# Last mixer of a two-model kernel: convolution taps added up by accumulating DMAs, all weights split, keys turned inside the value products

## The chip, the cores and the metric

The kernel runs on one core of a Trainium2 chip. Its time is the device time of one execution, in microseconds; the median of three executions before the change is 1564.31 us (1563.68 to 1568.18). A profiled execution of its own has a trace with the start and the duration of every instruction on every engine. The engines are named as in a profile: PE (TensorE's matmuls), PEld (its weight loads), DVE (VectorE), ACT (ScalarE), POOL (GpSimd) and SP (SyncE, which issues the weight loads from HBM).

## The reference

Two transformer-like models run one after the other on 256 tokens of width 1024: the first has two layers, the second has one layer, whose mixer is the last mixer of the program. It is the only part that the change touches:

```python
z = _rmsnorm(h, mix_norm[i]) @ w_in[i]
conv_a, conv_gt, q, k, v, r, g_lr = jnp.split(z, SPLIT_POINTS, axis=-1)
y_conv = _conv_module(conv_a, conv_gt, conv_w[i], conv_b[i], conv_ln_g[i], conv_ln_b[i])
y_gla = _gla(q, k, v, r, g_lr, gate_w_up[i], gate_b[i], gla_norm[i])
h = h + jnp.concatenate([y_conv, y_gla], axis=-1) @ w_out[i]
```

`_conv_module` forms `glu = a * sigmoid(b)` in 512 channels, runs a causal convolution of 31 taps along the tokens in each channel by itself, adds a bias, and applies a layer norm and SiLU. `_gla` is a gated linear attention in chunks of 64 tokens with four heads: decays are the exponential of a running sum of log-sigmoids, scores are taken inside each chunk, a state is handed from chunk to chunk, and its output has a norm and a gate `silu(r)`.

## The kernel before

All weights lie in one flat HBM tensor, in units of 128 x 1024 float32 (512 KB). SP loads one unit after the other into five staging buffers (tile `st`, line 179). A unit is normally *split* for an exact product in the fast format of PE: ACT casts it to the high half (`whi`, L158), DVE subtracts that from the unit and leaves the low half (`wlo`, L161), and activations are split likewise. A product of a weight block with the activations is then three matmuls (`mm3`: high by high, high by low, low by high; L276 to L278). The halves have seven buffers each. In the last mixer some units are used *raw*: the staged float32 block is multiplied directly with a float32 copy of the normalised input (`n.f32`, eight ACT instructions, L1159), one float32 matmul in place of three (L273, L348). The value weights and the output gate's weights are raw (`RAW_V`, `RAW_R`), the query and key weights are split.

The mixer runs in this order: eight units for `conv_a` and `conv_gt`, four times two (`conv_in` then forms `glu` for 128 channels, a quarter of them); one unit for the low-rank decay gate; two for queries and two for keys; four value units (`vproj`); the scores of four heads; the keys turned (four transposes of `ke` on PE, copied to `kt` by ACT, L1248 and L1249); three state products (L1256); the first half of the output gate (`output_gate(0)`, L273); the products of scores and states with values (L1307, L1311); the second half of the gate with the norm of the attention's output between its blocks (`o_norm`: column sums on PE, a power on POOL, L497; `o_scale`: eight diagonal matrices made by ACT, L506, and spread by PE, L516); then `w_out`, first with the four attention parts (`ys[4]` to `ys[7]`), then with the four convolution parts.

The taps of the convolution are background work, in a list `b.bg`; each weight unit that is asked for takes `b.rate` entries from it. Of 31 taps, DVE does 19 for each quarter in `tap`, each on top of the sum so far (`yc`, L1151; the first is ACT's, L1148). The other 12 (`NA`) are multiplied by ACT (`tap2`, two instructions for two quarters, L1143), and DVE adds the product to `yc` (L1144). When the second part of `w_out` is asked for, what is left in the list is issued and `conv_norm` follows: `centre` (column sums over the channels by PE, L1276; subtract, L1278; squares, L1280), `variance` (L483, a power, two diagonals), `scale` (L1291, SiLU L1292, split L372 and L373).

The order on each engine isn't that of the code: a scheduler at build time puts instructions of all engines in an order by when it expects them to be ready. On the chip each engine runs its list in that order and an instruction that waits holds up all behind it. Chores (`b.after`) are issued when so many blocks of matmuls have been issued. POOL runs three powers in this mixer and one small load.

Of the kernel before, what the change touches and what calls it, by code (L numbers as in the profile page):

```python
# [19 lines left out]
P = 128  # L20
# [14 lines left out]

RATE, R_QK, R_V, R_R, R_O, NA = 5, 5, 9, 10, 5, 12

RAW_QK, RAW_V, RAW_R = False, True, True

CONV_AT, CONV_WAIT, CONV_SQ, CONV_RMS = 1, 0, 6, 6  # L40
GATE_AT, O_SUM, O_SPREAD = 12, 4, 6

# [25 lines left out]
class Norm:  # L68
# [3 lines left out]
    def __init__(self, b, h2, finish):  # L72
        self.b, self.h2, self.finish = b, h2, finish
        self.f32 = None
        self.sq = [None, None]
        self.state = 0
        self.gap = 12
        self.waiting = []

    def __call__(self, k):  # L80
        return self.h2[:, k, :, :], self.f32 and self.f32[:, k, :]

# [42 lines left out]
class Builder:  # L125
# [38 lines left out]
    def wtile(self):  # L164
        return tuple(self.wpool.tile([P, UW], F32R, tag=t, name=t) for t in ("whi", "wlo")) + (None,)

# [8 lines left out]

    def unit(self, *slabs, raw=False):

        st, src = self.staged(slabs)
        self.nc.sync.dma_start(st, src)
        if raw:  # L180
            self.run_bg(self.raw_rate)
            return None, None, st
        w = self.wtile()
        self.halves(st, w, slice(0, UW))
        self.run_bg()
        return w
# [62 lines left out]

    def colunit(self, name, l, cols, raw=False):  # L250
        return self.unit(*self.colspec(name, l, cols), raw=raw)

# [9 lines left out]

    def vunit(self, name, l, u, c0, raw=False):
        return self.unit(raw=raw, *[(name, l, slice(k * P, (k + 1) * P), slice(c0, c0 + 512)) for k in (2 * u, 2 * u + 1)])


    def mm3(self, ps, w, b, a, first, last):

        hi, lo, raw = w
        s = slice(b * P, (b + 1) * P)  # L270
        mm = self.nc.tensor.matmul
        if raw is not None:
            mm(ps, raw[:, s], a[1], start=first, stop=last, skip_group_check=True)  # L273
        else:
            a = a[0]
            mm(ps, hi[:, s], a[:, 0, :], start=first, stop=False, skip_group_check=True)  # L276
            mm(ps, hi[:, s], a[:, 1, :], start=False, stop=False, skip_group_check=True)  # L277
            mm(ps, lo[:, s], a[:, 0, :], start=False, stop=last, skip_group_check=True)  # L278
        self.tick()

    def mmw(self, bank, w, b, a, first, last):


        hi, lo, _ = w
        s = slice(b * P, (b + 1) * P)
        a = a[0]
        mm = self.nc.tensor.matmul
        mm(bank[:, 0, :], lo[:, s], a[:, 0, :], start=first, stop=False, skip_group_check=True)  # L288
        mm(bank, hi[:, s], a, start=False, stop=last, skip_group_check=True)  # L289
        self.tick()  # L290
# [39 lines left out]

    def vproj(self, name, l, c0, h, raw=False):

        banks = [self.psw.tile([P, 512], F32, tag="bank", name="bank") for _ in range(2)]
        mm = self.nc.tensor.matmul
        for u in range(ND // 2):
            hi, lo, w = self.vunit(name, l, u, c0, raw)
            order = [(kk, t) for kk in range(2) for t in range(2)]
            if u == ND // 2 - 1:
                order.sort(key=lambda kt: kt[1])
            for kk, t in order:  # L340
                k = 2 * u + kk
                a2, a = h(k)
                ah, al = a2[:, 0, :], a2[:, 1, :]
                c = slice(kk * 512, (kk + 1) * 512)
                first, last = k == 0, k == ND - 1
                s = slice(t * P, (t + 1) * P)
                if raw:
                    mm(banks[t], a[:, s], w[:, c], start=first, stop=last)  # L348
                    continue
                mm(banks[t], ah[:, s], hi[:, c], start=first, stop=False)  # L350
                mm(banks[t], ah[:, s], lo[:, c], start=False, stop=False)  # L351
                mm(banks[t], al[:, s], hi[:, c], start=False, stop=last)  # L352
                self.tick(2)
# [14 lines left out]
    def split(self, src, name="a"):  # L368
# [4 lines left out]
        nc.vector.tensor_tensor(a[:, 1, :], src, a[:, 0, :].bitcast(F32), op=ALU.subtract)  # L373
        return a, None

# [123 lines left out]

    def diags(self, col, n, act=False):  # L500

        dg = []
        for i in range(n):
            d = self.small.tile([P, P], F32, tag="dg", name="dg")
            if act:
                self.nc.scalar.mul(d, self.ident, col[:, i:i + 1])  # L506
            else:
                self.spread = self.nc.vector.tensor_scalar_mul(d, self.ident, col[:, i:i + 1])
            dg.append(d)
        return dg  # L510

    def bcast(self, dg):

        ps = self.psw.tile([P, 512], F32, tag="bank", name="bank")
        for i, d in enumerate(dg):
            self.nc.tensor.matmul(ps[:, i * P:(i + 1) * P], self.ones, d, start=True, stop=True)  # L516
        return ps[:, 0:len(dg) * P]

# [121 lines left out]
def two_block_kernel(ctx: ExitStack, tc: tile.TileContext, x_in, mem_in, p_in, params, sinks, table, onehot,  # L640
# [360 lines left out]
    def embedding():  # L1001
# [3 lines left out]
        for k in range(2):  # L1005
            a = b.work.tile([P, 2, T], F32R, tag="sum", name="pk", bufs=4)
            nc.scalar.copy(a[:, 0, :], pin[:, k, :])
            nc.vector.tensor_tensor(a[:, 1, :], pin[:, k, :], a[:, 0, :].bitcast(F32), op=ALU.subtract)
            pk.append((a, None))
        pu.extend(b.rowunit("ple_w_proj_2", 0, slice(k * P, (k + 1) * P)) for k in range(2))  # L1010
# [7 lines left out]
    with tc.tile_pool(name="ple", bufs=1) as pp:  # L1018
# [4 lines left out]
        def products(bank, t, h, w, c, first, last):  # L1023
            s = slice(t * P, (t + 1) * P)
            ah, al = h[0][:, 0, s], h[0][:, 1, s]
            mm(bank, ah, w[0][:, c], start=first, stop=False)
# [76 lines left out]
def _gla_mixer(b, n, n2, gain, x, gate_up, cst, updater):  # L1103
# [3 lines left out]
    with b.acts(8), tc.tile_pool(name="gla", bufs=1) as gp:  # L1107
# [8 lines left out]
        nc.gpsimd.memset(reset[:, :, 0:1], 0.0)  # L1116
        n.f32 = gp.tile([P, ND, T], F32, tag="h32", name="h32")

        def cu(c, raw=False):
            return b.colunit("w_in_2", 0, slice(c, c + P), raw)  # L1120


        glu = gp.tile([P, 4, T + NT - 1], F32, tag="glu", name="glu")
        nc.gpsimd.memset(glu[:, :, 0:NT - 1], 0.0)
        yc = gp.tile([P, 4, T], F32, tag="yc", name="yc")
        cw = gain("conv_w_2", 4 * NT)
        cb = gain("conv_b_2", 4)

        def conv_in(i, bank):
# [4 lines left out]
            nc.vector.tensor_tensor(glu[:, i, NT - 1:], t[:, 0, :], sg, op=ALU.mult)  # L1134
            b.bg += [lambda j=j: tap(i, j) for j in range(NT - NA)]
            if i % 2:
                b.bg += [lambda j=j: tap2(i - 1, j) for j in range(NT - NA, NT)]

        def tap2(i, j):

            t = gp.tile([P, 2, T], F32, tag="tap", name="tap", bufs=2)
            for e in range(2):
                nc.scalar.mul(t[:, e, :], glu[:, i + e, j:j + T], cw[:, 4 * j + i + e:4 * j + i + e + 1])  # L1143
            nc.vector.tensor_tensor(yc[:, i:i + 2, :], yc[:, i:i + 2, :], t, op=ALU.add)  # L1144

# [9 lines left out]
        for i in range(4):  # L1155
            bank = b.proj([cu(o + i * P) for o in (0, 512)], n, kouter=(i == 0))[0]
            n.then(lambda i=i, bank=bank: conv_in(i, bank))
        for d in range(ND):
            nc.scalar.mul(n.f32[:, d, :], x[:, d, :], gain("mix_norm_2")[:, d:d + 1])  # L1159


        b.rate = b.raw_rate = R_QK
        ug = b.unit(*[("w_in_2", 0, slice(k * P, (k + 1) * P), (2560, 16)) for k in range(ND)])
# [37 lines left out]
        k = b.work.tile([P, 2, T], F32, tag="sum", bufs=4, name="k")  # L1201
        bank = b.proj([cu(1024 + e * P, RAW_QK) for e in range(2)], n)[0]
        nc.vector.scalar_tensor_tensor(q, bank, 0.125, b.rb2(n), op0=ALU.mult, op1=ALU.mult)
        bank = b.proj([cu(1280 + e * P, RAW_QK) for e in range(2)], n)[0]
        nc.vector.tensor_tensor(k, bank, b.rb2(n), op=ALU.mult)
# [4 lines left out]
        qd, qu, kd, ku, ke = (prods[i] for i in ("qd", "qu", "kd", "ku", "ke"))  # L1210


        b.rate = b.raw_rate = R_V
        v = gp.tile([P, 2, 512], F32, tag="v", name="v")
        for t, bank in enumerate(b.vproj("w_in_2", 0, 1536, n, RAW_V)):
            nc.scalar.mul(v[:, t, :], bank, n.rt[:, t:t + 1])
# [4 lines left out]
        def output_gate(i):  # L1221
            bank = b.proj([cu(2048 + (2 * i + e) * P, RAW_R) for e in range(2)], n)[0]
            rr = b.work.tile([P, 2, T], F32, tag="sum", bufs=4, name="gu")
# [15 lines left out]
        for h in range(4):  # L1239
            scores(h)  # L1240
        b.rate = b.raw_rate = R_R


        kt = gp.tile([P, 2, 2, P], F32, tag="t1", name="kt")
        ps = b.psw.tile([P, 2, 2, P], F32, tag="bank", name="bank")
        for t in range(2):
            for a in range(2):
                nc.tensor.transpose(ps[:, t, a, :], ke[:, a, t * P:(t + 1) * P], b.ident)  # L1248
        nc.scalar.copy(kt, ps)  # L1249
        st = gp.tile([P, 3, 2, P], F32, tag="state", name="state")  # L1250
# [71 lines left out]
        def o_scale(rt):  # L1322
            for i in range(2):
                ps = b.bcast(b.diags(rt[:, 4 * i:4 * i + 4], 4, act=True))
                for e in range(2):
# [12 lines left out]
        def part(j, i):  # L1338
            def f():
                b.rate = R_O  # L1340
                w = b.rowunit("w_out_2", 0, slice(i * P, (i + 1) * P))
                if j == CONV_AT:
                    b.run_bg(len(b.bg))
                    conv_norm()
# [98 lines left out]
```

## Time and profile before

| | |
|---|---|
| median of three executions | 1564.31 us |
| the profiled execution's own time | 1567.1 us |
| its span from the first instruction to the last | 1565.3 us |
| PE busy in the span | 1541.1 us |
| DVE busy | 1211.2 us |
| ACT busy | 884.2 us |
| POOL busy | 28.1 us |
| share of the chain that ended last: PE, DVE, ACT | 94%, 3%, 2% |

A row names the line, the engine, the operation and the tiles (out<-in). Times of a stretch are counted from the span's start. PE's matmuls overlap, so a row's duration is longer than the distance between two starts. The granted clock of PE is 1.00 at 2.4 GHz; at its lower level, 1.2 GHz, it would be 0.5, and a stretch with both lies between. The last mixer takes PE from about 1224.6 us to 1341.8 us, where the next feed-forward's first matmul starts.

### The profile page before, as it was taken

What the parts mean: (1) busy time and instruction counts of PE and PEld (TensorE: products, weight loads), DVE (VectorE), ACT (ScalarE), POOL (GpSimd) and SP (SyncE); (2) the same over time, 40 slices, a digit from 0 to 9 for tenths busy, and PEclk for the clock granted to TensorE, in tenths of its full rate; (3) what the DMA queues carried; (4) which work ended last, traced back from release to release, by engine and by line L of the source; (5) the groups of instructions that cost most, each with busy time, mean ns of one, the idle gap of its engine ahead of it and who ended that gap; (6) DMA issues with size and microseconds to landing.
All of it is one profiled execution on the core that took longest, in us unless ns stands there. A gap on an engine that the chain in (4) does not pass through costs nothing.

```text
span 1565.3 us, 23488 instructions
## 1 busy us (share of the span) xinstructions
PE 1541.1 (98%) x8896; PEld 1341.4 (86%) x8896; DVE 1211.2 (77%) x2039; ACT 884.2 (56%) x1530; POOL 28.1 (2%) x41
## 2 busy tenths in 40 slices
PE   8999999999999999999999999999999999999997
PEld 7888887888888888888788888888888968888886
DVE  7977788878776787778687877778776897877774
ACT  7555546556555555554655655555555557555553
POOL 1000000000000000000000000000000000000000
PEclk9999999999999999999999999999999999999999
DMA  8655464427554666547352755447554524565542
GB/s 285 217 182 189 158 219 135 161 98 252 191 192 133 212 217 195 191 144 242 133 179 87 245 188 188 139 167 247 188 183 142 203 73 142 172 219 189 195 153 90
DMA packets 78418, 279.11 MB, mean 178 GB/s; under 512 B 8986, under 2 KB 10042, under 8 KB 78304
## 3 DMA queue, kind: packets, MB, share of 16 engines
q1 hardware_dynamic: 76176, 273.19, 52.7%
q0 software_dynamic: 1120, 3.36, 0.6%
q8 instruction: 70, 1.15, 0.3%
q10 hardware_dynamic: 1008, 1.05, 0.2%
q14 instruction: 44, 0.36, 0.1%
HBM read 276.50 MB, written 1.07 MB: 177 GB/s over the span
## 4 chain that ended last, share of the span: by engine, by line
PE 94%; DVE 3%; ACT 2%; DMA 1%; issue 0%; POOL 0%; ACTq 0%; POOLq 0%; SPq 0%; DVEq 0%
PE bank L289 44%; PE bank L288 23%; PE abank L289 9%; PE abank L288 5%; DMA st<-wflat 1%; PE bank L350 1%; PE bank L348 1%; PE bank L352 1%; PE bank L351 1%; PE bank L276 1%; PE bank L277 1%; PE bank L278 1%; PE bank L273 1%; DVE x L679 1%; PE bank L483 0%; PE bank L516 0%
## 5 line engine op out<-in xcount | busy, mean ns | idle before, releaser
L289 PE MATMUL bank<-h,whi 128*128 128x512 f32 x2416 | 847.3, 393 | 0.0
L288 PE MATMUL bank<-h,wlo 128*128 128x256 f32 x2416 | 679.4, 281 | 7.2 <-DVE wlo L161 7.2
L161 DVE TENSOR_TENSOR wlo<-st,whi 128x1024 fp32r<-128x1024 f32 (+1 forms) x515 | 612.7, 1208 | 63.0 <-ACT whi L158 62.6
L158 ACT CAST whi<-st 128x1024 fp32r<-128x1024 f32 (+1 forms) x515 | 532.2, 1041 | 152.5 <-DMA st<-wflat 97.4
L289 PEld LDWEIGHTS bank<-h,whi 128*128 128x128 f32 x2416 | 452.1, 187 | 100.4 <-DVE h L432 0.3
L288 PEld LDWEIGHTS bank<-h,wlo 128*128 128x128 f32 x2416 | 456.5, 189 | 12.1 <-DVE wlo L161 6.8
L327 ACT COPY sum<-bank 128x256 f32<-128x256 f32 x310 | 114.1, 370 | 284.9 <-PE bank L289 284.5
L289 PE MATMUL abank<-a,whi 128*128 128x512 f32 x624 | 222.2, 393 | 0.0
L328 DVE TENSOR_TENSOR sum<-bank,sum 128x256 f32<-128x256 f32 x310 | 130.3, 423 | 113.4 <-ACT sum L327 112.8
L289 PE MATMUL bank<-a,whi 128*128 128x512 f32 x624 | 218.1, 393 | 0.0
L288 PE MATMUL bank<-a,wlo 128*128 128x256 f32 x624 | 175.0, 281 | 0.0
L288 PE MATMUL abank<-a,wlo 128*128 128x256 f32 x624 | 174.8, 282 | 0.0
L289 PEld LDWEIGHTS bank<-a,whi 128*128 128x128 f32 x624 | 116.8, 187 | 26.4
L289 PEld LDWEIGHTS abank<-a,whi 128*128 128x128 f32 x624 | 116.7, 187 | 26.0
L288 PEld LDWEIGHTS bank<-a,wlo 128*128 128x128 f32 x624 | 117.9, 189 | 1.4 <-DVE pt L618 0.8
L288 PEld LDWEIGHTS abank<-a,wlo 128*128 128x128 f32 x624 | 117.6, 189 | 1.0 <-issue 0.8
L546 DVE TENSOR_TENSOR sum<-sum,rb 128x512 f32<-128x512 f32 x132 | 90.8, 691 | 3.4
L372 ACT CAST a<-a 128x256 fp32r<-128x256 f32 x132 | 53.3, 407 | 55.9 <-DVE a L550 55.8
L373 DVE TENSOR_TENSOR a<-a,a 128x256 fp32r<-128x256 f32 x132 | 55.1, 421 | 26.8 <-ACT a L372 26.7
L548 ACT ACTIVATE sg<-sum 128x256 f32<-128x256 f32 x132 | 54.4, 415 | 32.3 <-DVE sum L546 32.2
L550 DVE TENSOR_TENSOR a<-sg,sum 128x256 f32<-128x256 f32 x132 | 55.0, 420 | 7.4 <-ACT sg L548 6.8
L679 DVE SCALAR_TENSOR_TENSOR x<-bank,x 128x256 f32<-128x256 f32 x80 | 33.1, 421 | 35.0 <-PE bank L289 34.0
(273 smaller groups left out, 1240.7 us busy)
## 6 DMA issues: line engine op xcount, KB each, us to landing
st<-wflat SPq DMA_DIRECT2D x515, 512.0 KB, 4.2
tb<-fd POOLq DMA_DIRECT2D x4, 512.0 KB, 4.0
x<-x_in SPq DMA_DIRECT2D x4, 256.0 KB, 4.4
mem<-mem_in SPq DMA_DIRECT2D x4, 256.0 KB, 8.7
st<-wflat ACTq DMA_DIRECT2D x4, 128.0 KB, 5.9
st<-wflat SPq DMA_DIRECT2D x4, 128.0 KB, 4.0
gf<-last_gain POOLq DMA_DIRECT2D x1, 512.0 KB, 5.5
out_dram<-y ACTq DMA_DIRECT2D x2, 256.0 KB, 2.6
```

Of the source, the lines that this page charges most:

```text
L158: hi = self.nc.scalar.copy(w[0][:, s], st[:, s])
L161: lo = self.nc.vector.tensor_tensor(w[1][:, s], st[:, s], w[0][:, s].bitcast(F32), op=ALU.subtract)
L288: mm(bank[:, 0, :], lo[:, s], a[:, 0, :], start=first, stop=False, skip_group_check=True)
L289: mm(bank, hi[:, s], a, start=False, stop=last, skip_group_check=True)
L327: self.nc.scalar.copy(dst, banks[c][:, 1, :])
L328: self.nc.vector.tensor_tensor(dst, banks[c][:, 0, :], dst, op=ALU.add)
L372: nc.scalar.copy(a[:, 0, :], src)
L373: nc.vector.tensor_tensor(a[:, 1, :], src, a[:, 0, :].bitcast(F32), op=ALU.subtract)
L546: nc.vector.tensor_tensor(gu, gu, self.rb2(n), op=ALU.mult)
L548: nc.scalar.activation(sg, gu[:, 0, :], AF.Silu)
L550: nc.vector.tensor_tensor(a, sg, gu[:, 1, :], op=ALU.mult)
L679: nc.vector.scalar_tensor_tensor(x[:, d, :], bank[:, e, :], scale, x[:, d, :], op0=ALU.mult, op1=ALU.add)
```

## The change

Of the 31 taps ACT now multiplies 18 and DVE 13. DVE no longer adds ACT's products: the first product of each pair of quarters is written straight into a tile `yd`, and each of the other 17 goes into one of four buffers `tap`, from which a DMA issued by POOL adds it to `yd` in SBUF. The two pairs have a `yd` each, so there are 2 x 17 such DMAs, and each waits for the one before it on the same `yd`. `conv_rest` adds both `yd` to `yc` at the end. No unit is raw any more, so the value and gate weights are split by ACT and DVE and take three matmuls a block, and `n.f32` goes. The keys are turned by a chore inside the value products. The eight diagonals of the output norm become two DVE instructions of 128 x 512 and two matmuls of that width. The rates at which background work is issued are lower.

```diff
-RATE, R_QK, R_V, R_R, R_O, NA = 5, 5, 9, 10, 5, 12
-RAW_QK, RAW_V, RAW_R = False, True, True
+RATE, R_QK, R_V, R_R, R_O, NA = 3, 2, 4, 5, 5, 18
-GATE_AT, O_SUM, O_SPREAD = 12, 4, 6
+GATE_AT, TURN_AT, O_SUM, O_SPREAD = 12, 16, 6, 5
...
+        yd = [gp.tile([P, 2, T], F32, tag=f"yd{p}", name="yd") for p in range(2)]
+        taps2 = [[], []]
...
-            b.bg += [lambda j=j: tap(i, j) for j in range(NT - NA)]
+            b.bg += [lambda j=j: step(i, j) for j in range(NT - NA)]
             if i % 2:
-                b.bg += [lambda j=j: tap2(i - 1, j) for j in range(NT - NA, NT)]
-        def tap2(i, j):
-            t = gp.tile([P, 2, T], F32, tag="tap", name="tap", bufs=2)
+                taps2[i // 2].extend(range(NT - NA, NT))
+        def step(i, j):
+            tap(i, j)
+            p = max(range(2), key=lambda p: len(taps2[p]))
+            if taps2[p]:
+                tap2(p, taps2[p].pop(0))
+        def conv_rest():
+            b.run_bg(len(b.bg))
+            for p in range(2):
+                while taps2[p]:
+                    tap2(p, taps2[p].pop(0))
+            for p in range(2):
+                ycp = yc[:, 2 * p:2 * p + 2, :]
+                nc.vector.tensor_tensor(ycp, ycp, yd[p], op=ALU.add)
+        def tap2(p, j):
+            t = yd[p] if j == NT - NA else gp.tile([P, 2, T], F32, tag="tap", name="tap", bufs=4)
             for e in range(2):
-                nc.scalar.mul(t[:, e, :], glu[:, i + e, j:j + T], cw[:, 4 * j + i + e:4 * j + i + e + 1])
-            nc.vector.tensor_tensor(yc[:, i:i + 2, :], yc[:, i:i + 2, :], t, op=ALU.add)
+                i = 2 * p + e
+                nc.scalar.mul(t[:, e, :], glu[:, i, j:j + T], cw[:, 4 * j + i:4 * j + i + 1])
+            if t is not yd[p]:
+                nc.gpsimd.dma_start(yd[p], t, accum_op=ALU.add)
...
-        for d in range(ND):
-            nc.scalar.mul(n.f32[:, d, :], x[:, d, :], gain("mix_norm_2")[:, d:d + 1])
...
+        def turn():
+            ps = b.psw.tile([P, 2, 2, P], F32, tag="bank", name="bank")
+            for t in range(2):
+                for a in range(2):
+                    nc.tensor.transpose(ps[:, t, a, :], ke[:, a, t * P:(t + 1) * P], b.ident)
+            nc.scalar.copy(kt, ps)
+        b.after(TURN_AT, turn)
...
-                ps = b.bcast(b.diags(rt[:, 4 * i:4 * i + 4], 4, act=True))
+                dg = gp.tile([P, 4, P], F32, tag="odg", name="dg", bufs=2)
+                nc.vector.tensor_tensor(dg, b.ident.unsqueeze(1).to_broadcast([P, 4, P]),
+                                        rt[:, 4 * i:4 * i + 4].unsqueeze(2).to_broadcast([P, 4, P]), op=ALU.mult)
+                ps = b.bcast([dg.rearrange("p c q -> p (c q)")], 4 * P)
...
                 if j == CONV_AT:
-                    b.run_bg(len(b.bg))
+                    conv_rest()
                     conv_norm()
```

The scheduler moves instructions as well. On POOL, in the last mixer before, two powers (`r<-v`, with 8 and 2 columns) follow each other with nothing between them:

```order
L1116 MEMSET reset_12478 128x8
L497 TENSOR_TENSOR r_12550<-v_12549,mhalf_88 128x2
L497 TENSOR_TENSOR r_13300<-v_13299,mhalf_88 128x8
L497 TENSOR_TENSOR r_13448<-v_13447,mhalf_88 128x2
```

After, on the same place of POOL, 34 accumulating DMAs stand among them; `yd_12484` is the first pair of quarters and `yd_12485` the second. These are the rows around the 8-column power, of which 22 DMAs stand ahead of it and 12 behind it:

```order
L1147 DMA yd_12485<-tap_12998 128x512
L1147 DMA yd_12484<-tap_13083 128x512
L1147 DMA yd_12485<-tap_13073 128x512
L484 TENSOR_TENSOR r_13423<-v_13422,mhalf_88 128x8
L1147 DMA yd_12485<-tap_13078 128x512
L1147 DMA yd_12484<-tap_13111 128x512
L1147 DMA yd_12485<-tap_13088 128x512
L1147 DMA yd_12484<-tap_13121 128x512
```

From the start of the list the DMAs stand thus: nine on the first pair; two times one on the second pair and one on the first; seven on the second; one on each; the power; five times one on each; two on the second; the 2-column power.

On ACT the decay (from `z`, the gate's pre-activation, to `eend`, the last of its exponentials) stood in one piece before:

```order
L1181 ACTIVATE z<-bank,pc 128x256 x2
L1183 ACTIVATE az<-z 128x512
L1184 ACT_TABLE_LOAD
L1184 ACTIVATE az<-az 128x512
L1185 ACT_TABLE_LOAD
L1185 ACTIVATE az<-az 128x512
L1194 ACT_TABLE_LOAD
L1194 ACTIVATE epos<-cum 128x512
L1195 ACTIVATE eneg<-cum 128x512
L1197 ACTIVATE eend<-dl 128x512
```

After, four pairs of taps and three casts stand inside it (the three exponentials `epos`, `eneg` and `eend` follow the last row):

```order
L1182 ACTIVATE z<-bank,pc 128x256
L1145 ACTIVATE tap<-glu,pc 128x256 x2
L1182 ACTIVATE z<-bank,pc 128x256
L156 CAST whi<-st 128x1024
L1184 ACTIVATE az<-z 128x512
L1145 ACTIVATE tap<-glu,pc 128x256 x2
L1185 ACT_TABLE_LOAD
L1185 ACTIVATE az<-az 128x512
L1145 ACTIVATE tap<-glu,pc 128x256 x2
L1186 ACT_TABLE_LOAD
L1186 ACTIVATE az<-az 128x512
L156 CAST whi<-st 128x1024 x2
```

On PE the convolution's norm (L1276 is the centring, L483 the variance's sums, L516 the spreading of the scale) had the attention's `w_out` products (`abank`) after the centring and between its later steps. Of 96 such products all stood behind the centring:

```order
L516 MATMUL bank<-dg,ones 128x128 x3
L1276 MATMUL bank<-yc,ones 128x256
L516 MATMUL bank<-dg,ones 128x128
L1276 MATMUL bank<-yc,ones 128x256
L516 MATMUL bank<-dg,ones 128x128 x2
L1276 MATMUL bank<-yc,ones 128x256 x2
L276 MATMUL abank<-a_13350,whi 128x256 x4
```

After, the first pair's centring (L1282) stands 13 products ahead of their end, and the second pair's centring, the sums (L470) and the spreading (L500) follow each other with no product between them, ahead of the first convolution part (`a_13609`):

```order
L267 MATMUL abank<-a_13485,whi 128x256
L268 MATMUL abank<-a_13485,whi 128x256
L269 MATMUL abank<-a_13485,wlo 128x256
L1282 MATMUL bank<-yc,ones 128x256 x2
L470 MATMUL bank<-ones,sq 128x1 x8
L500 MATMUL bank<-dg,ones 128x128 x2
L267 MATMUL abank<-a_13609,whi 128x256 x4
```

## Rows read from the trace of the kernel before

**Rows 1.** The page's busy times: engine, us, share of the span, instructions.

```profile
PE 1541.1 (98%) x8896; PEld 1341.4 (86%) x8896; DVE 1211.2 (77%) x2039; ACT 884.2 (56%) x1530; POOL 28.1 (2%) x41
```

**Rows 2.** Windows of the mixer: stretch, its length, busy time of each engine, granted clock, DMA.

```profile
1278.30:1284.40 6.10, 4.46 (x61) 3.93 (x61) 6.10 (x16) 4.47 (x9) 0.00 (x0) 1.00 0.24 87
1284.40:1305.40 21.00, 21.00 (x111) 18.30 (x112) 16.87 (x38) 8.71 (x19) 2.01 (x1) 0.92 0.29 102
1305.40:1316.60 11.20, 8.03 (x37) 6.77 (x36) 8.54 (x17) 11.20 (x27) 0.00 (x0) 0.85 0.38 139
```

**Rows 3.** Chain that ended last, inside the mixer: start us, us, what (merged).

```profile
1247.48 0.12 PE bank L276
...
1264.56 13.75 PE bank L348 x32
1278.33 3.34 DMA st<-wflat
...
1284.37 8.79 PE bank L273 x32
...
1302.65 2.02 POOL r L497
...
1305.39 4.13 ACT tap L1143 x10
...
1313.94 0.85 PE bank L1276 x2
```

**Rows 4.** Timeline of PE, split products 512 columns wide: start us, us.

```profile
1000.24 0.39 PE L289 MATMUL abank<-a,whi 128*128 128x512 f32 x1
1000.47 0.28 PE L288 MATMUL abank<-a,wlo 128*128 128x256 f32 x1
```

**Rows 5.** Groups by line from 1243 to 1316.6, ACT, then DVE: busy, mean, idle.

```profile
L1143 ACT ACTIVATE tap<-glu,pc 128x256 f32<-128x256 f32 x48 | 21.2, 499 | 4.4 <-DVE yc L1144 4.1
L158 ACT CAST whi<-st 128x1024 fp32r<-128x1024 f32 x7 | 7.2, 1041 | 9.5 <-DMA st<-wflat 9.5
...
L1151 DVE SCALAR_TENSOR_TENSOR yc<-glu,pc,yc 128x256 f32<-128x256 f32 x72 | 30.4, 478 | 0.1
L1144 DVE TENSOR_TENSOR yc<-yc,tap 128x512 f32<-128x512 f32 x24 | 16.4, 682 | 1.1 <-ACT tap L1143 0.7
```

**Rows 6.** Timelines of ACT and DVE up to the decayed keys.

```profile
1242.21 0.73 ACT L1133 ACTIVATE sg<-gu 128x256 f32<-128x256 f32 x2
...
1257.21 0.84 ACT L1181 ACTIVATE z<-bank,pc 128x256 f32<-128x256 f32 x2 [3.23 <-PE bank L1177]
...
1266.13 0.61 ACT L1197 ACTIVATE eend<-dl 128x512 f32<-128x512 f32 x1
...
1272.57 0.67 DVE L1209 TENSOR_TENSOR ke<-k,eend 128x512 f32<-128x512 f32 x1
```

**Rows 7.** DMA issues of the program: size each, median us from issue to landing.

```profile
tb<-fd POOLq DMA_DIRECT2D x4, 512.0 KB, 4.0
...
out_dram<-y SPq DMA_DIRECT2D x2, 256.0 KB, 2.4
pin<-p_in POOLq DMA_DIRECT2D x1, 256.0 KB, 4.5
...
gup<-gate_up POOLq DMA_DIRECT2D x1, 16.0 KB, 2.0
```

**Rows 8.** Timelines of DVE and PE from the convolution's centring to the mixer's end.

```profile
1317.82 1.08 DVE L1278 SCALAR_TENSOR_TENSOR yc<-bank,yc 128x256 f32<-128x256 f32 x3
...
1323.36 0.16 DVE L493 TENSOR_SCALAR v<-bank 128x2 f32<-128x2 f32 x1 [1.19 <-PE bank L483]
...
1325.65 1.22 DVE L161 TENSOR_TENSOR wlo<-st,whi 128x1024 fp32r<-128x1024 f32 x1
...
1329.24 0.75 DVE L373 TENSOR_TENSOR a<-yc,a 128x256 fp32r<-128x256 f32 x2
...
1341.68 0.28 PE L278 MATMUL abank<-a,wlo 128*128 128x256 f32 x1
```

## The prediction before the run

> **What bounds the kernel now.** I read the busy times first: PE is busy for 98% of the span [rows 1], so outside the stretches where it waits or runs at a lower clock, only less work for PE saves time. Second the windows of the mixer [rows 2]: there PE does wait. In 1278.3 to 1284.4 it is busy for 4.46 of 6.10 us, in 1305.4 to 1316.6 for 8.03 of 11.20, and the clock granted around these gaps is 0.92 and 0.85 instead of 1.00. Third the chain that ended last [rows 3] for what released PE: a weight load of 3.34 us at 1278.33, held back by raw units in the staging buffers, and ten ACT taps (4.13 us) at 1305.39 that stand ahead of the diagonals of the output norm. Fourth the groups by line [rows 5]: DVE spends 30.4 us on its own taps and 16.4 us on adding ACT's products. The last place to read is the end [rows 8]: between the centring and the mixer's last product at 1341.96 (1341.68 + 0.28) PE has no gap, since the attention's part of `w_out` covers the convolution's norm.
>
> **PE, part by part.** The raw values take 13.75 us [rows 3]. Split, they are 16 blocks of three products 512 wide, which start 0.23 us apart (1000.47 - 1000.24 [rows 4]): 48 x 0.23 = 11.0, so -2.7. Half of the raw gate takes 8.79 us, both halves 17.6; split, 32 blocks of three at 0.12 [rows 3] are 11.5, so -6.1. The two waits are worth 6.10 - 4.46 = 1.6 and 11.20 - 8.03 = 3.2, and the clock 0.08 x 21.0 + 0.15 x 8.03 = 2.9. All of it together is -16.5 us. That is the most that PE can give back; the wide diagonals trade eight small matmuls for two wide ones and I cost them at nothing, beside the longer waits below.
>
> **ACT and DVE.** ACT gets 24 more taps (72 instead of 48, 21.2 / 48 = 0.44 us each: 10.6) and 8 more casts at 1.04 [rows 5] (8.3). In 1305.4 to 1316.6 it is already busy without a pause [rows 2]. DVE loses 24 taps x 0.478 = 11.5 and 24 additions = 16.4 [rows 5]; it gets 8 low halves x 1.22 [rows 8] = 9.8 and four instructions of the size of an addition (two sums, two diagonals, 4 x 0.68 = 2.7), so it is 15.4 us freer. DVE no longer limits anything. ACT's eight float32 copies stood in waits for loads; I cost their end at nothing.
>
> **The decay comes later.** Four pairs of taps (8 x 0.44 = 3.5) and three casts (3.1) now stand between `z` and `eend`, which took from 1257.21 to 1266.74 [rows 6]; that is 6.6 us, of which a part falls into waits that ACT had there anyway. I take 4 (bounds 2 and 6.6). The keys `ke` are then ready at 1273.24 + 4 = 1277.2. Their transposes now stand in PE's list behind 31 of the 48 value products, which PE reaches at 1264.56 + 31 x 0.23 = 1271.7: a new wait of 5.5 us inside the values.
>
> **The accumulating DMAs are the term that decides.** The first is ready when ACT has finished its two sigmoids (1242.94 [rows 6]), a cast (1.04), an identity (taken as a tap, 0.5) and four taps (1.8): 1246.2. Each waits until the one before it on the same `yd` has landed, and POOL takes them in its list's order, so the 34 make 9 + 2 + 7 + 1 + 5 + 2 = 26 steps in a row; the other eight run beside one of the other pair. A tap buffer is free only when its DMA has landed, and ACT's casts queue behind a tap that waits for one, so a long step slows ACT's whole list, and PE with it, and isn't made up for elsewhere. What a step costs no row shows, since before no DMA accumulates. From POOL's queue 16 KB land in 2.0 us and 512 KB in 4.0 [rows 7]: 2.0 us for 496 KB more, hence 2.0 + 1.0 = 3.0 for the 256 KB of a step, if it were a copy. The destination has to be read as well: between nothing and 1.0 more. The ends: 2.4, the 256 KB that leave SBUF on idle queues at the program's end, and 4.5, 256 KB from POOL's queue beside weight loads [rows 7]. I take 3.3: the row of POOL's own queue with a third of the second read, because SBUF is the source. The convolution's sum is then complete at 1246.2 + 26 x 3.3 = 1332.0.
>
> The Trainium skill (Collectives: The Full Stack, "The bandwidth ceiling: the fold count and why AG ≠ RS ≠ AR") says that an addition in a DMA isn't slowed by the adder but by its two source reads, which about halve the rate of a copy; no run here shows that yet. By it a step would be 2.0 + 2.0 = 4.0 and the time 1594.7.
>
> **What follows the sum, and the total.** PE's list has nothing left to cover the norm behind the second pair's centring. The last addition (0.68), two centring matmuls (0.85 [rows 3]), four subtractions (1.08 / 3 = 0.36 each, 1.5) and the last square with its sum (0.8, estimated from the taps) are 3.8; from `v` to the first low half took 1323.36 to 1329.6, 6.3 us, in which DVE placed two low halves of weights of 1.2 us that cost about half a step each [rows 8]: 5.1. Together 9.0 us. Then 32 blocks of the convolution's part, 32 x 0.36 = 11.5, and the clock after so long a gap, as in 1284.4 to 1305.4: 1.7. The mixer ends at 1332.0 + 9.0 + 11.5 + 1.7 = 1354.2 instead of 1341.96, +12.2 us. All earlier gains of PE lie beside the chain of DMAs. The profiled execution took 1567.1 us, so it would take 1579.3; the median of the runs is 2.8 us below that execution: 1564.31 + 12.2 = 1576.5. For the chain alone the break-even step is 3.3 - 12.2 / 26 = 2.83 us.
>
> **Rivals.**
> *No change: ACT's list and the power on POOL set the end.* The output norm's power stands in POOL's list with 12 of the DMAs, 7 steps, behind it. It started at 1302.65 [rows 3]; values -2.7, first gate half 5.8 - 8.79 = -3.0, the wait for the weights -1.6, the late keys +5.5, and 11 split gate blocks ahead of its sums instead of 4 raw ones (11 x 0.36 - 4 x 0.55 = +1.8) leave it at 1302.7. With steps of 2.5, 1302.7 + 2.0 + 7 x 2.5 = 1322.2, + 22.2 = 1344.4: +2.4, 1566.7. Up to steps of 3.1 this end is later than the chain's, and up to 2.8 it comes to no more than +4.5. For it speaks the full ACT in [rows 2], against it only the price of a step: the 3.0 of POOL's own row.
> In a sentence of its own: the Trainium skill (DMA: Bandwidth & Descriptors, "Anatomy of one DMA — SWDGE (gpsimd) path") gives 2.0 us plus the bytes at 436 GB/s, 2.6 for a step, which would put the chain's end at 1313.8 and make this rival the result; the 2.0 agrees with the 16 KB row, while the 512 KB row is 0.8 above the formula.
>
> *Faster: the DMAs hide.* If the steps stay at or below 2.5 us, so that the sum is there when PE has done the attention's part of `w_out`, and the decay isn't late, PE sets the end: -16.5 + 9.0 + 1.7 = -5.8, 1558.5. For it: DVE is freed and the two waits in [rows 2] lose their causes. Against it: both conditions have to hold, and the only row at 2.5 is one of idle queues and another queue's making.
>
> **How the numbers follow.** About 0.3% (4.7 us) is what a measurement of this kernel can tell from no change. The forecast, steps of 2.8 us and more with the chain of DMAs as the end from 3.1 on, has 0.60: it gives slower by more than that. ACT and the power: 0.20, no change. PE alone: 0.20, faster. The predicted time is the forecast's 1576.5; its own range is 1569 (steps of 2.8) to 1595 (4.0), and 1608 would be steps of 4.5. With the two rivals the range is 1557 to 1597.
>
> **What the profile of the changed kernel would show.** The accumulating DMAs of one pair start over 3 us apart, in a row, from about 1246 on, and ACT's taps wait for them. PE waits inside the values for `ke`, near 1272. The addition of the second `yd` comes at about 1332, PE then has a gap of some 9 us ahead of the convolution's part, and the clock falls behind it. DVE's busy share in the mixer falls. The forecast is wrong if a step is under 2.8 us, if `yd` is complete before PE has finished the attention's part of `w_out`, or if ACT's taps never wait.

## The result: 1614.01 us, 3.1% slower

The changed kernel takes 1614.01 us (median of 4 runs, 1608.19 to 1615.64), the kernel before 1564.99 us (4 runs): a ratio of 1.0306, interval 1.0287 to 1.0325. The forecast was 1576.5 us with a range of 1557 to 1597: slower was right, but by 49 us and not by 12. The profiled execution took 1614.28 us, its span is 1612.5 us and its mean granted clock 0.981 (before: 0.997).

The busy times of the whole execution answer to [rows 1]. PE's busy time grew by only 10 us, while the span grew by 47. PE waits more.

```profile
PE 1551.1 (96%) x8932; PEld 1354.2 (84%) x8932; DVE 1200.1 (74%) x2003; ACT 895.7 (56%) x1546; POOL 56.0 (3%) x75
```

The windows of the mixer show where, with the columns of [rows 2]; the last stretch ends where the following feed-forward layer starts, at 1389.1 instead of 1341.8. The 47 us are all here.

```profile
1264.40:1278.30 13.90, 7.32 (x27) 5.69 (x26) 5.04 (x7) 8.26 (x14) 2.53 (x3) 0.75 0.71 200
1278.30:1284.40 6.10, 2.89 (x13) 2.06 (x11) 2.08 (x3) 4.93 (x7) 1.55 (x2) 0.94 0.33 57
1284.40:1305.40 21.00, 15.21 (x120) 13.62 (x121) 15.65 (x35) 15.26 (x29) 6.08 (x8) 0.77 0.74 151
1305.40:1316.60 11.20, 8.73 (x65) 7.78 (x63) 8.05 (x11) 2.71 (x5) 1.70 (x2) 1.00 0.88 253
1316.60:1341.50 24.90, 15.08 (x69) 13.07 (x70) 8.56 (x18) 15.28 (x33) 9.41 (x10) 0.66 0.62 126
1341.50:1364.40 22.90, 13.01 (x83) 11.87 (x81) 6.28 (x7) 8.90 (x16) 6.00 (x7) 0.78 0.84 199
1364.40:1389.10 24.70, 19.49 (x121) 18.31 (x122) 9.13 (x23) 7.89 (x20) 0.72 (x1) 0.72 0.00 1
```

From 1264.4 to 1364.4 no engine is full: PE is busy for 62.2 of 100.0 us, DVE and ACT for less. Such a stretch is paced by a wait. The view of the tile `yd` (instructions, what they waited for, who waited for them) names it:

```profile
L1147 POOL DMA_DIRECT2D yd<-tap x34: 839/852/1180, 1246.6 to 1361.1; - x34
...
  POOL yd L1147: 75.7, 26
  ACT tap L1145: 43.2, 22
...
DMA to landing us min/median/max: 3.2/3.7/7.4
```

POOL stands for 75.7 us until the transfer before has landed; ACT stands for 43.2 us, in 22 waits, until a transfer frees a tap buffer. PE's waits, longest sums first, are the echo:

```profile
PE bank L470 <- ACT osq L1320: 9.4, 1, 9.4
PE bank L1220 <- DVE ke L1210: 9.0, 1, 9.0
PE bank L1282 <- DVE yc L1138: 8.5, 2, 5.9
PE bank L337 <- ACT z L1182: 6.6, 1, 6.6
```

The gate `z`, the keys `ke` and the squares `osq` all come out of ACT's list (`ke` by way of the exponentials), behind taps that wait for buffers. The sum `yc` is the chain of transfers itself. POOL's timeline (start, us, idle time before) shows its pace:

```profile
1246.58 0.94 POOL L1147 DMA_DIRECT2D yd<-tap  x1 [14.77 <-ACT tap L1145]
1251.31 0.86 POOL L1147 DMA_DIRECT2D yd<-tap  x1 [3.78 <-DMA yd<-tap]
1255.15 0.84 POOL L1147 DMA_DIRECT2D yd<-tap  x1 [2.98 <-DMA yd<-tap]
1258.95 0.84 POOL L1147 DMA_DIRECT2D yd<-tap  x1 [2.95 <-DMA yd<-tap]
1266.89 0.84 POOL L1147 DMA_DIRECT2D yd<-tap  x1 [7.10 <-DMA yd<-tap]
...
1283.70 0.85 POOL L1147 DMA_DIRECT2D yd<-tap  x1 [2.92 <-ACT whi L156]
1285.27 0.84 POOL L1147 DMA_DIRECT2D yd<-tap  x1 [0.72 <-ACT tap L1145]
1287.24 0.85 POOL L1147 DMA_DIRECT2D yd<-tap  x1 [1.13 <-DMA yd<-tap]
...
1326.52 0.85 POOL L1147 DMA_DIRECT2D yd<-tap  x1 [2.29 <-DMA yd<-tap]
1330.84 1.66 POOL L484 TENSOR_TENSOR r<-v,mhalf 128x8 f32<-128x8 f32 x1 [3.47 <-DVE v L480]
1332.47 1.78 POOL L1147 DMA_DIRECT2D yd<-tap  x2
```

With one accumulator in turn, starts lie 3.8 us apart when nothing else moves (1251.31, 1255.15, 1258.95) and once 7.94 beside three weight loads (1258.95 to 1266.89). Where the list alternates between the two accumulators (1283.70 to 1287.24) they lie under 2 us apart. The power at 1330.84 waits for its input and holds up the transfer behind it in POOL's list. The end of the chain that ended last shows the tail: last transfer, sum, the column sums of the squares, first product of the convolution.

```profile
1361.10 3.30 DMA yd<-tap
1364.42 0.70 DVE yc L1138
...
1367.84 3.59 PE bank L470 x16
...
1376.08 1.23 PE abank L267 x4
```

### The profile page after: what moved, and what is told of

Read it like the earlier page. It is cut to its first block, busy times and chain, and to the rows that moved or that the text cites. A ratio compares the mean times of both kernels' runs of the same rounds, so it can differ in the third digit from the quotient of the medians.

```text
span 1612.5 us, 23626 instructions
## 1 busy us (share of the span) xinstructions
PE 1551.1 (96%) x8932; PEld 1354.2 (84%) x8932; DVE 1200.1 (74%) x2003; ACT 895.7 (56%) x1546; POOL 56.0 (3%) x75
## 4 chain that ended last, share of the span: by engine, by line
PE 84%; DMA 6%; issue 3%; DVE 3%; ACT 2%; POOL 0%; ACTq 0%; POOLq 0%; SPq 0%; DVEq 0%
PE bank L279 41%; PE bank L278 22%; PE abank L279 9%; DMA yd<-tap 5%; PE abank L278 4%; DMA st<-wflat 1%; PE bank L337 1%; PE bank L339 1%; PE bank L338 1%; PE bank L470 1%; DVE wlo L159 1%; DVE x L663 1%; PE bank L799 0%; DVE h L419 0%; PE abank L769 0%
## 5 line engine op out<-in xcount | busy, mean ns | idle before, releaser
L159 DVE TENSOR_TENSOR wlo<-st,whi 128x1024 fp32r<-128x1024 f32 (+1 forms) x523 | 622.1, 1207 | 78.3 <-ACT whi L156 78.2
L156 ACT CAST whi<-st 128x1024 fp32r<-128x1024 f32 (+1 forms) x523 | 540.3, 1041 | 151.0 <-DMA st<-wflat 91.1
L278 PEld LDWEIGHTS bank<-a,wlo 128*128 128x128 f32 x624 | 117.8, 189 | 1.4 <-DVE pt L602 0.8
```

What stands on the lines that cost most here:

```text
L156: hi = self.nc.scalar.copy(w[0][:, s], st[:, s])
L159: lo = self.nc.vector.tensor_tensor(w[1][:, s], st[:, s], w[0][:, s].bitcast(F32), op=ALU.subtract)
```

## Experiments

Theory A: transfers to one accumulator wait for each other, and this chain sets the end. Rivals: B, the four tap buffers; C, contention with weight loads; D, the rest of the change.

**The sums alone (e6_raw).** On the kernel before:

```diff
-RATE, R_QK, R_V, R_R, R_O, NA = 5, 5, 9, 10, 5, 12
+RATE, R_QK, R_V, R_R, R_O, NA = 3, 2, 4, 5, 5, 18
+ step, conv_rest, tap2 with yd and accum_op (tap bufs=3)
```

> The kernel before with only the sums by transfers taken over from the change (18 taps of ScalarE, its list and its rates; three tap buffers, since four don't fit beside the unsplit operand); the weights that were unsplit before stay so, keys are turned and diagonals built as before. Theory A (26 serial steps of 4.5 us from 1246 on set the end whatever the products are): 1600 to 1620. Rival D (half of the loss is the splits' work): 1580 to 1592.

1613.49 us, ratio 1.0312 (1.0295 to 1.0330). The sums alone cost as much as the whole change. The last transfer is issued at 1360.7, as in the changed kernel (1361.1), although there are three tap buffers instead of four.

**Two accumulators a pair (e3_chains).**

```diff
+            k = (j - NT + NA) % 2
...
-                nc.gpsimd.dma_start(yd[p], t, accum_op=ALU.add)
+                nc.gpsimd.dma_start(yd[p][k], t, accum_op=ALU.add)
```

The edit also puts the wide diagonals into tiles that are free by then, as in e4 below.

> The changed kernel with two second accumulators for each pair of channel groups, taken in turn, so that a transfer waits for the one before the last of its pair; 32 transfers, two more VectorE additions of 0.69 us at the end; four tap buffers as before. Theory A with the step made of waiting (issue 0.85, landing 3.2, handoff 0.5, while bytes move for only about 1.6 us): transfers overlap two by two, the last one lands 25 to 40 us earlier and the kernel takes 1575 to 1590. If the bytes themselves (C) or the tap buffers (B) set the pace: above 1605.

1584.70 us, ratio 1.0131 (1.0116 to 1.0147), 29 us below the changed kernel. The transfers' lines:

```profile
L1149 POOL DMA_DIRECT2D yd<-tap x32: 839/847/1523, 1245.0 to 1304.1; - x32
...
DMA to landing us min/median/max: 3.2/4.3/8.7
```

Nearly the same bytes (32 transfers instead of 34) are issued 57 us earlier, although a transfer lands later (median 4.3 instead of 3.7 us). So the queue could carry them; it was the waiting for one accumulator that didn't let it. The program's order changed along with this: all 32 transfers now stand ahead of the power on POOL, which held the chain up by about 2 us in the changed kernel. PE's longest wait is now 11.5 us for `kd`. Of the 20 us left above the kernel before, the splits alone cost 14.5 (e9 below); the rest isn't taken apart.

**Seven tap buffers (e4_bufs).**

```diff
-tag="tap", name="tap", bufs=4)
+tag="tap", name="tap", bufs=7)
-tag="odg", name="dg", bufs=2)
+tag=("t1", "epos")[i], name="dg")
```

> The changed kernel with seven tap buffers instead of four (the wide diagonals lie in tiles that are free by then, to make room). Rival B (ScalarE's in-order list stands behind a tap buffer, 43 us in 22 waits, and with it the casts, the decay and TensorE): most of these waits go, and the kernel takes 1590 to 1600. Theory A (each transfer waits for the one before it on its accumulator, so the last one lands when 26 steps are over, however early the taps stand ready): the decay comes earlier and TensorE's waits for it shrink, but the last transfer still lands at about 1364 us and the kernel stays within 5 us of 1614.

1596.04 us in one run, 18 us below: what B expected, and against A as I had put it. The last transfer is issued at 1339.1 instead of 1361.1. The timeline of POOL shows why:

```profile
1265.98 1.71 POOL L1147 DMA_DIRECT2D yd<-tap  x2 [6.34 <-DMA yd<-tap]
...
1281.24 0.85 POOL L1147 DMA_DIRECT2D yd<-tap  x1 [0.94 <-DMA yd<-tap]
1283.04 0.84 POOL L1147 DMA_DIRECT2D yd<-tap  x1 [0.95 <-DMA yd<-tap]
```

With more buffers the program's order itself changes: 31 transfers instead of 22 stand ahead of the output norm's power on POOL, and from 1266 on many starts follow each other by under 2 us. From 1265.98 to 1321.86 there are 23 steps from one start to the next, 2.43 us each; in the changed kernel 14 from 1266.89 to 1318.68, 3.70 each. The first transfer also starts 4.7 us earlier (1241.88). So A and B needn't be rivals: as I read it, the buffers decide the order, and the order decides how early both accumulators are at work. Buffers and order change together here, so their shares aren't shown; that e6 ends as late with three buffers, and 23 transfers ahead of the power, speaks for the order.

**What a step is made of (e1_copy, e2_half, e8_quiet).**

```diff
e1  -  nc.gpsimd.dma_start(yd[p], t, accum_op=ALU.add)
    +  nc.gpsimd.dma_start(yd[p], t)
e2  -  nc.gpsimd.dma_start(yd[p], t, accum_op=ALU.add)
    +  nc.gpsimd.dma_start(yd[p][:, 0, :], t[:, 0, :], accum_op=ALU.add)
e8  -  self.nc.sync.dma_start(st, src)
    +  self.nc.sync.dma_start(st[:, 0:P], src[:, 0:P])
    ...
```

> The changed kernel with each of the 34 transfers as a plain copy of the tap tile onto the sum tile, in the same order and with the same waits; what the copies overwrite is not added, so the convolution's sums are left out. Theory A (the serial chain of 26 accumulating steps sets the end, and a step costs 3.8 us alone because a destination tile is read as well as written): a lone copy lands in about 2.5 us instead of 3.2, a step is about 3.1, the 26 steps are shorter by 13 to 20 us, and the kernel takes 1594 to 1601. Rival C (weight loads on the same DMA engines make the step long, reading the destination costs nothing): a copy lands as late as an accumulating transfer, the time stays within 5 us of 1614.

> The changed kernel with each of the 34 transfers carrying 128 x 256 elements (128 KB) instead of 128 x 512; the other half of each tap tile is left out of the sum. Theory A by bytes: lone landing falls from 3.2 to about 2.4 us, a step from 3.8 to 3.0, 26 steps from 118 to about 85 us, the kernel to about 1582. A by fixed cost (issue, waiting and write receipt): landing about 3.0, the kernel above 1605. Rival B (the four tap buffers stall ScalarE's list, whatever a transfer takes) moves with the landing as A does, but its gain stays under 10 us.

> The changed kernel with weight loads of 64 KB instead of 512 KB from the gate unit to the mixer's end; the splits read the 128 loaded columns eight times over, so all engine work stays and the mixer's values aren't the reference's. Theory C (weight loads on the same DMA engines lengthen a step from 3.8 to 4.5): the 34 transfers land within 3.5 us each, the chain takes 26 x 3.8 = 99 us instead of 118, the kernel 1593 to 1598. Theory A without contention (a step is long by its own handling): the largest landings stay above 5 us and the time within 5 us of 1614.

One run each: 1596.45, 1590.91 and 1599.27 us; e1 as A had it, e8 1.3 us beyond C's range. The bytes moved in a transfer that runs by itself, first accumulating (changed kernel, 40 slices of 0.1 us from 1251.0), then two copies (40 slices of 0.2 us from 1250.5):

```profile
GB/s 0 0 0 0 0 0 0 0 0 0 0 0 0 0 0 0 0 164 164 225 205 184 205 164 205 205 184 205 164 225 123 0 0 0 0 0 0 0 0 0
```

```profile
GB/s 0 0 0 0 0 0 0 0 0 451 348 389 123 0 0 0 0 0 0 0 0 0 0 307 430 389 185 0 0 0 0 0 0 0 0 0 0 307 348 328
```

Adding moves 164 to 225 GB/s, copying 300 to 450. The Trainium skill (Collectives: The Full Stack, "The bandwidth ceiling: the fold count and why AG ≠ RS ≠ AR") says of collectives that the two source reads of a reduction about halve the rate of a copy; these rows agree (bytes move for 1.4 us instead of about 0.7). Bytes move in 1.4 of the 3.8 us of a lone accumulating step. The lone transfers on the chain, of the changed kernel, of copies and of halves:

```profile
1255.15 3.27 DMA yd<-tap
```

```profile
1254.04 2.27 DMA yd<-tap
```

```profile
1251.78 2.67 DMA yd<-tap
```

To each come 0.5 us until POOL's next issue. Half the bytes save 0.60 us, so about 2.1 of the 3.27 us depend on no byte (3.27 - 2 x 0.60). A copy is 1.0 us shorter: 0.3 of it is POOL's issue (0.54 instead of 0.85 us), 0.7 the rate. With one eighth of the mixer's later weight bytes (e8) the transfers' lines read:

```profile
L1156 POOL DMA_DIRECT2D yd<-tap x34: 839/854/1178, 1244.3 to 1346.2; - x34
...
DMA to landing us min/median/max: 3.2/3.4/6.0
```

From first issue to last landing it is 105.2 us instead of 117.8 (1346.2 + 3.3 - 1244.3, 1361.1 + 3.3 - 1246.6): 12.6 of its gain of 14.7 us. C is a part, not the whole. How large a part is known from below only, since seven loads of 512 KB, for the layer behind, still run from 1304 on (the changed kernel has 22 from 1240 to 1365). For e2, A's bound by bytes (1582) was missed, as the fixed part is larger than I had put it, and so was B's (a gain under 10 us; it was 23).

**The rest of the change (e5_dve, e9_split, e12_values, e13_gates).**

```diff
e5   after:  - nc.gpsimd.dma_start(yd[p], t, accum_op=ALU.add)
             + nc.vector.tensor_tensor(yd[p], yd[p], t, op=ALU.add)
     -RATE, R_QK, R_V, R_R, R_O, NA = 3, 2, 4, 5, 5, 18
     +RATE, R_QK, R_V, R_R, R_O, NA = 3, 2, 4, 5, 5, 12
e9   after, with tap2, NA = 12 and the rates 5, 5, 9, 10, 5 of before
e12  before: - RAW_QK, RAW_V, RAW_R = False, True, True
             + RAW_QK, RAW_V, RAW_R = False, False, True
e13  before: - RAW_QK, RAW_V, RAW_R = False, True, True
             + RAW_QK, RAW_V, RAW_R = False, True, False
```

> The rest of the change without its transfers: all weights split, keys turned inside the value products, wide diagonals, and the sums of ScalarE's 12 taps (as before) added by VectorE to the second accumulator. Theory A (all of the loss is the transfers'): between 1550 and 1567, ratio to the kernel before 0.99 to 1.002. Rival D (the splits of 12 more weights and the turned keys delay the mixer by themselves): over 1580, ratio above 1.01.

> All weights split, keys turned inside the value products and wide diagonals as in the changed kernel; the convolution as in the kernel before (12 taps of ScalarE, VectorE adds them, 5, 5, 9, 10, 5 chores a unit). The run with 19 taps on VectorE under the sparse rates of the change (1587.94) left a flush of about 20 us of taps to the mixer's end, so it doesn't price the splits. Theory A (the loss is the way ScalarE's taps are summed): 1556 to 1570. Rival D (12 more splits, 1.14 us of VectorE and 0.95 us of ScalarE each, delay taps and decay): VectorE, already at 84 us of 99 in the mixer, gets 13.7 us more and becomes the bound, 1575 to 1590.

> The kernel before with the weights of the values alone split (48 products of 512 columns in place of 32, four casts and four VectorE subtractions more); the output gates' weights stay unsplit and the sums are as before. The prediction's term for the values was 13.75 us down to 48 x 0.23 = 11.0: by it 1562 to 1565. Rival D, after the run with all weights split (there a product of 512 columns took 0.43 us, at a granted clock of 0.65 to 0.78): 48 x 0.43 = 20.6 us instead of 13.9, 1570 to 1576.

> The kernel before with the weights of the output gates alone split (96 products of 256 columns in place of 64, four casts and four subtractions more). The prediction's term was 17.6 us down to 11.5: by it 1558 to 1562. Rival D (VectorE's and ScalarE's lists are late there, and the clock falls where TensorE waits): 1566 to 1573.

All four are slower than before by 0.6 to 1.5%, as D had it or beyond: e5 1587.94 us (ratio 1.0149, 1.0126 to 1.0172), e9 1579.15 (1.0092, 1.0077 to 1.0107), e12 1579.33 (1.0074, 1.0048 to 1.0101), e13 1575.58 (1.0055, 1.0037 to 1.0073). e5 keeps the change's sparse rates and so flushes taps at the mixer's end; it says little on the splits. e9 has 8 splits more than the kernel before (523 low halves against 515), not the 12 of its expectation. e12 changes one flag. Windows of the kernel before and of e12:

```profile
1264.00:1278.30 14.30, 14.30 (x38) 6.36 (x36) 14.24 (x26) 10.95 (x24) 0.00 (x0) 1.00 0.35 112
```

```profile
1264.00:1278.30 14.30, 10.07 (x60) 8.26 (x58) 14.30 (x26) 8.88 (x19) 0.00 (x0) 0.77 0.15 50
1278.30:1284.40 6.10, 5.18 (x12) 4.12 (x13) 5.96 (x11) 4.46 (x11) 0.00 (x0) 0.50 0.27 86
```

DVE was full here before (14.24 of 14.30 us), and a split adds a low half to it for each weight. In e12 the low half of the first value unit comes at 1263.1 and the next at 1278.0, with taps, sums and the decayed keys between them in DVE's list. The build put the scores, which need `kd`, and the turning of the keys between the 14th and the 15th value product. PE now waits for both:

```profile
PE abank L1234 <- DVE kd L1209: 3.8, 1, 3.8
...
PE bank L351 <- DVE wlo L161: 1.4, 1, 1.4
```

The first 14 products start 0.23 us apart at the full clock. Around the waits the granted clock is 0.77, and then 0.50, its lower level of 1.2 GHz, where products start 0.43 us apart (1280.67, 1281.10); from 1285.3 on they are 0.23 apart again.

Values, scores and turning together take PE from 1264.9 to 1290.1, 25 us; before, they took 17 (1264.6 to 1281.6). e13 shows the lower clock at the gates, but behind another wait:

```profile
PE bank L1256 <- ACT kt L1249: 3.6, 1, 3.6
```

```profile
1284.40:1305.40 21.00, 17.15 (x92) 15.19 (x93) 17.47 (x38) 6.78 (x14) 0.00 (x0) 0.53 0.37 125
```

There PE waits for ACT and not for a low half: the copy of the turned keys (`kt`) starts at 1286.05, behind two weight casts from 1284.17, and a wait of 5.9 us for `a`, also ACT's, follows at the end of the gates.

**Attempts at a faster version (e7_turn, e10_mix).**

```diff
e7   before: + turn() ahead of the scores; wide diagonals on DVE
e10  e3 with NA = 8, rates 5, 4, 6, 8, 8:
     - if taps2[p]:
     + if taps2[p] and j % 3 == 0:
```

> The kernel before with only the keys turned ahead of the scores and the wide diagonals built by VectorE. The waits of the kernel before for the turned keys (1.6 us) and for ScalarE's diagonals (3.2 us) go: 1560 to 1565, a ratio of 0.997 to 1.000. If VectorE's list takes the place of ScalarE's: within 2 us of 1565.6 on either side.

> A version meant to relieve both lists: all weights split and keys turned as in the change, ScalarE takes 8 of 31 taps (12 before, 18 in the change), summed by 12 transfers on four accumulators, one tap pair at every third chore; 5, 4, 6, 8, 8 chores a unit. Against the run with all weights split (1579.15, VectorE is late there) VectorE has 16 more taps of 0.40 us but 24 fewer additions of 0.69 us and 4 more at the end, 7 us less in sum, and ScalarE 16 fewer taps of 0.49 us. If VectorE's and ScalarE's lists are what the splits cost: 1560 to 1572. If the transfers cost something beyond their own chain (their issue, or contention with weight loads): over 1575.

e7: 1564.16 us, ratio 1.0003 (0.9990 to 1.0015), no change. e10: 1580.38 us in one run. Its 12 transfers are all issued by 1266.5 and hold up nothing more, but PE waits 5.0 us for `kd` and 4.2 for a low half: so what the splits cost is, as I read it, left. No version was faster than the kernel before.

## Why the prediction was right in direction and wrong in size

**The accumulating DMAs (the step that failed).** The mechanism held: first transfer at 1246.58 (predicted 1246.2), each behind the one before on its accumulator, taps and PE held up. The term was mis-sized: "I take 3.3" for a step. From first issue to last landing are 117.8 us, which is 4.53 for each of 26 steps, and 26 x (4.53 - 3.3) = 32 us is nearly all of the error of 35 us in the mixer's end (1389.2 against 1354.2). A lone step is 3.8: I priced the landing (3.27) and left out the 0.5 us until POOL issues the next. That the landing fits is luck: a copy lands in 2.27 and not 3.0, and adding costs 1.0 more (0.3 of it at POOL's issue) and not 0.3. Weight loads add another 12.6 / 26 = 0.5 on average, or more (e8). Of the last 0.25, 6.4 us in sum, the power on POOL explains about 2: the transfers on the second pair ahead of it and behind it start 5.95 us apart (1326.52, 1332.47). The rest I can't assign. The bound of 4.5 [rows 7], a transfer of 256 KB beside weight loads, was the nearer row for a stretch in which weight loads run most of the time.

**26 steps.** The count fits this kernel's order but is no constant: with seven tap buffers the order was another and the end 22 us earlier, 4.7 of them by an earlier start (e4).

**The decay.** Predicted: 4 us later, keys at 1277.2, PE waits 5.5 us. `eend` starts at 1287.34 instead of 1266.13 [rows 6], and PE waits 9.0 us. I counted the instructions that were put in front; the tap waits on the transfers, which I had named, I did not add to this term.

**PE.** "The most that PE can give back", -16.5 us, shows in no run. With the sums left on DVE the splits cost time: 0.92% together (e9), 0.74 and 0.55% each half alone. The distance of 0.23 us in [rows 4] was right at the full clock (e12). What the term left out are PE's waits for `kd`, low halves, `kt` and `a` out of DVE's and ACT's lists, and the lower clock around them. These three runs keep DVE's 19 taps and its additions, which the change takes away; with DVE freed and two accumulators a pair (e3), PE waits 11.5 us for `kd`. So whether the credit can be had where DVE has time and the decay is early stays open. In the changed kernel none of this shows, since the chain is longer still: with the weights unsplit it takes as long (e6). That term was off the path, as I said, and so were the loads of the engines: DVE is 11.1 us less busy, not 15.4, and ACT 11.5 more, not 18.9 (10.6 + 8.3).

**The tail.** Predicted 9.0 us from the sum to the convolution's first product and 13.2 to the mixer's end: 11.7 (1376.08 - 1364.42) and 13.1. The longest piece of it is the column sums of the squares, 3.59 us, where I had 0.8 for the last square and its sum.

**Rivals.** The power on POOL came at 1330.84 and not at 1302.7, as its squares wait in ACT's list; transfers went on behind it. No change needed steps under 2.8 us, faster steps of 2.5 at most; a lone accumulating step is 3.8, and even a plain copy comes to 2.77 (2.27 + 0.5, e1).

**Turned keys and wide diagonals**, costed at nothing or at removed waits of 4.8 us: no effect (e7).

## What to carry to other kernels

Price a chain of dependent transfers from issue to issue under the traffic of its own stretch, not by one landing on a quiet queue, and count how many accumulators are in work at once; a second accumulator a pair costs one addition and took back 29 of the 49 us, in an order that changed along with it. Before crediting TensorE with cheaper products, look whether the engines that make its operands have time left in that window: where they hadn't (e12, e13), TensorE waited, and then ran at the lower clock.

## What was unexpected

An accumulating transfer occupies POOL for 0.85 us at its issue, a plain copy of the same tile for 0.54, and halving the bytes changes nothing in that (0.85). And a number of buffers changed the order of another engine's list: POOL had 31 instead of 22 transfers ahead of the same power.
